# Inverting the tiles of a whole head with pairs of tiles as diagonal blocks of one 128-column stationary operand

## The chip, the cores and the metric

The kernel runs on one core of one Trainium2 chip. The metric is the device time of one launch in microseconds (us), the median over several runs; a lower number is better. Everything said of the hardware here is read from the profile of the kernel's own execution.

## The reference

The program is a two-layer decoder trunk on 1024 positions of width 1024. The first layer mixes positions with a gated DeltaNet of 8 heads (head size 128), the second with a state-space layer ("S5") of 64 groups of 16 channels; beside each runs a cross-attention into 256 memory tokens, and after each comes an MLP with 4096 hidden channels. Two pieces matter here.

In the DeltaNet, each head's sequence is cut into chunks, and each chunk needs the inverse of a unit lower triangular matrix:

```
a_strict = where(strict, einsum('bhnid,bhnjd->bhnij', kb, k) * decay, 0)
sol = triangular_solve(eye + a_strict, rhs, left_side=True, lower=True, unit_diagonal=True)
...
state, o = scan over chunks   # each chunk uses its part of sol
```

The kernel works with chunks of 128 positions, so a head has 8 such 128x128 matrices ("tiles"). In the S5 layer the output of a position has a skip term, `y = y + d_skip * u`.

## The kernel before, in words

All large products are split into a high and a low part (fp32r) and take three matmuls (lines L367 to L369, in `mm3`). The small products of the DeltaNet and the S5 set-up are plain fp32 matmuls; in the trace each of them appears as two MATMUL records and two LDWEIGHTS records.

The program first loads x, projects keys, computes the memory attention, and then goes through the 8 DeltaNet heads. For a head h, `gdn_recur(h)` (the scan over the 8 tiles) is woven with `gdn_fill(h + 1)`, which projects queries, values and the gate of the next head (and keys of the head after) and, between the projection steps, inverts the tiles of head h + 1 (`gdn_invert_tiles`). After the last head follow the output projection, the MLP, the S5 layer and the second MLP. In the first MLP, `s5_side` prepares the S5 matrices beside the large products (`s5_mats`, 16 calls).

The inverses of the 32x32 diagonal blocks of the tiles are computed on VectorE by `gdn_inverse`, for two heads at a time (0 and 1, 2 and 3, ...), and left in DRAM (`t32`, plain and transposed; `ntf` holds the negated strict part of the tiles). `gdn_invert_tiles` joins these blocks: first two 32-blocks to a 64-block, then two 64-blocks to the 128-tile. Each join is a product of the off-diagonal block with the two inverses. Before the change it goes through the four tiles of one half of a head (`hf` = 0, then 1) in five steps; each step, `mm4`, is a group of four matmuls, one for each tile, with 64 stationary and 64 moving columns into one PSUM bank (tag `pi`, one buffer, shared with the transposes `ot`), followed by one or two small copies on ScalarE and VectorE that place the result for the next step. Ten such groups make a head, 80 the program. Names: `lead`, `unit` and `pair` are three 128x512 tiles in the buffers `h4` (six of them), made once at the start and called `bd` in the profile; `nt` holds the off-diagonal blocks; `TT` (called `iv`, as the PSUM bank is too) receives the inverse and is read by `gdn_recur`.

In `s5_mats`, `pz` is a product of four matmuls with 16 stationary columns (one group of channels each) and 128 moving ones; the skip term, a 16x16 diagonal from `dd`, is added to it, and the 16 rows go to DRAM (`zd`) in one transfer of the GpSimd queue.

The order of the instructions on every engine is not that of the code. When the whole program has been recorded, `settle` plans it: each instruction has a cost (`price`) and a due time, TensorE may take matmuls up to 40 us ahead of their turn (`reach=40`), and every engine is then given its order as a chain. Within its engine an instruction then waits for those ahead of it. Tiles of one tag are given out in the recorded order.

Of the kernel before, what the change touches and what calls it, by code (L numbers as in the profile page):

```python
# [30 lines left out]
class Trunk:  # L31
# [26 lines left out]
    def settle(self, first, last, reach=0.0, ahead=15.0, passes=1, margin=0.0, late=0.0, hold=1e3):  # L58
# [10 lines left out]
        ins = traced[k0:k1]  # L69
        n = len(ins)  # L70
# [39 lines left out]
        reads, writes, users, fresh, cost, port = {}, {}, {}, [], [], []  # L110
# [709 lines left out]
    def gdn_consts(self):  # L820
        nc = self.nc
        scr = self.tile("scr", [P, 9 * P], F32, "scr")[:, :P + 8 + 13 * 64 + 96]
        self.small = [scr[:, P + 8 + n * 64:P + 8 + (n + 1) * 64] for n in range(13)]
        early = self.tile("h1", [P, 3 * P], F32, "early")
        U = early[:, 0:P]
        nc.gpsimd.memset(U, 1.0)
        nc.gpsimd.affine_select(U, U, [[1, P]], ALU.is_ge, 0.0, base=0, channel_multiplier=-1)
        self.U = U
        ones = early[:, P:2 * P]
        nc.gpsimd.memset(ones, 1.0)  # L830
        self.ones = ones
        mn = scr[:, 0:P]
        nc.gpsimd.memset(mn, 0.0)
        nc.gpsimd.affine_select(mn, mn, [[1, P]], ALU.is_ge, -1e30, base=0, channel_multiplier=-1)
        self.maskneg = mn
        self.early = [early[:, 2 * P + 64 * n:2 * P + 64 * (n + 1)].rearrange("p (t h) -> p t h", t=8) for n in range(2)]
        self.lead, self.unit, self.pair = (self.tile("h4", [P, 4, P], F32, "bd") for _ in range(3))
        for o in (self.lead, self.pair):
            nc.gpsimd.memset(o, 0.0)
        nc.gpsimd.memset(self.unit, 0.0)  # L840
        for r, c in ((0, 0), (32, 64), (64, 32)):
            nc.scalar.copy(self.unit[r:r + 32, :, c:c + 32], self.ident[r:r + 32, r:r + 32].unsqueeze(1).to_broadcast([32, 4, 32]))
# [285 lines left out]
    def blocks(self, o, h, hf, w, places):  # L1128

        for b, c in places:  # L1130
            q = slice(32 * b, 32 * b + 32)
            self.nc.sync.dma_start(o[q, :, c:c + 32], self.t32[w, h, 4 * hf:4 * hf + 4, b].rearrange("t i c -> i t c"))

    def gdn_invert_tiles(self, h):

        nc = self.nc
        V = nc.vector
        T32, zi = self.lead, self.unit
        B = self.pair.rearrange("p t (w c) -> p w t c", w=2)
        A, B = B[:, 0], B[:, 1]  # L1140

        def mm4(a, b):
            ps = self.psum("pi", "iv", (P, 4, P))[:64, :, 0:64]
            for t in range(4):
                nc.tensor.matmul(ps[:, t], a[:, t], b[:, t], start=True, stop=True)
            return ps

        out = self.TT[h] = []
        for hf in range(2):
            NT = self.tile("h4", [P, 4, P], F32, "nt")  # L1150
            for o, c, w in ((0, 64, 64), (64, 32, 32)):
                nc.sync.dma_start(NT[:, :, o:o + w], self.ntf[h, hf][:, :, c:c + w])
            TT = self.tile("h3", [P, 4, P], F32, "iv")
            nc.gpsimd.memset(TT, 0.0)
            self.blocks(T32, h, hf, 0, ((0, 0), (2, 32)))
            self.blocks(TT, h, hf, 1, ((0, 0), (1, 32), (2, 64), (3, 96)))
            out.append(TT)
            ps = mm4(NT[:, :, 32:96], T32[:, :, 0:64])
            nc.scalar.copy(zi[32:64, :, 0:32], ps[32:64, :, 0:32])
            V.tensor_copy(zi[96:128, :, 32:64], ps[0:32, :, 32:64])  # L1160
            yield 0.5
            ps = mm4(TT[:, :, 0:64], zi.rearrange("p t (w c) -> p t w c", c=32)[:, :, 0:3:2])
            nc.scalar.copy(A[0:64], ps)
            yield 0.5
            ps = mm4(zi[:, :, 0:64], TT.rearrange("p t (w c) -> p t w c", c=32)[:, :, 1:4:2])
            nc.scalar.copy(TT[0:32, :, 32:64], ps[0:32, :, 0:32])
            V.tensor_copy(TT[64:96, :, 96:128], ps[32:64, :, 32:64])
            yield 0.5
            ps = mm4(NT[:, :, 0:64], A)
            nc.scalar.copy(B[64:128], ps)  # L1170
            yield 0.5
            ps = mm4(B, TT[:, :, 64:128])
            nc.scalar.copy(TT[0:64, :, 64:128], ps)
            yield 0.5

    def gdn_queries_out(self, h, hf):

# [533 lines left out]
    def s5_mats(self, m, b, co, banks):  # L1711

        nc = self.nc
# [8 lines left out]
        dd = self.dd(8 * m + 4 * b)  # L1722
        pz = self.psum(banks[0], "pz", (P, 4, 8, 16))
        for g in range(4):
            nc.tensor.matmul(flat(pz[:16, g]), co[:, 0, 4 * b + g, :], flat(h1[:, g]), start=True, stop=True)
        z = self.tile("h5", [P, 4, 8, 16], F32, "z")[:16]
        nc.scalar.copy(z[:, :, 1:8], pz[:16, :, 1:8])
        V.tensor_tensor(z[:, :, 0], pz[:16, :, 0], dd, op=ALU.add)  # L1728
        nc.gpsimd.dma_start(self.zd[m, :, gs, 112:], z.rearrange("p g e o -> p g (e o)"))
# [82 lines left out]
    def s5_read(self, m, u, rs, M0, H):  # L1812

        nc = self.nc
        for b, r in enumerate(rs):
# [9 lines left out]
    def dd(self, g0):  # L1825

        nc = self.nc
        o = self.tile("S", [P, 4, 16], F32, "dd")
        nc.vector.tensor_tensor(o[:16], self.ident[:16, :16].unsqueeze(1).to_broadcast([16, 4, 16]),
                                self.dsk[:, g0:g0 + 4].unsqueeze(2).to_broadcast([16, 4, 16]), op=ALU.mult)  # L1830
        return o[:16]

    def glu(self):
        nc = self.nc
# [194 lines left out]
    def run(self):  # L2029
        nc = self.nc  # L2030
        a = self.a
        d = lambda n, shape: self.dp.tile(shape, F32, tag=n, name=n)
        self.dsk = self.const("dsk", [16, 64])
        nc.sync.dma_start(self.dsk, a["dskT"])
        self.gdn_consts()
        self.s5_scratch()

        self.cat = d("cat0", [1536, T])
# [153 lines left out]
def layouts(x):  # L2192
# [33 lines left out]
    o["dskT"] = c(x["s5_d"].reshape(64, 16).T)  # L2226
# [25 lines left out]
```

## Time and profile before

| | before |
|---|---|
| median of 3 runs | 2619.41 us (2617.07 to 2619.64) |
| profiled execution: time / span | 2622.83 us / 2621.1 us |
| mean granted TensorE clock | 0.993 |
| TensorE matmul busy | 2553.5 us (97%) |
| VectorE / ScalarE / GpSimd busy | 1929.3 us (74%) / 1304.3 us (50%) / 338.1 us (13%) |

In the rows of the profile, PE is TensorE's matmuls, PEld its weight loads, DVE VectorE, ACT ScalarE, POOL GpSimd and SP SyncE, which issues most transfers; a name with a q at its end (SPq, POOLq) is the sequencer of that engine. A row of the timeline gives the start, the length, the engine, the line and operation, the tiles written and read, the size of the operand and the count of equal instructions that were merged. "128*64 128x64" in a matmul row means 128 rows by 64 stationary columns, and a moving operand of 128 partitions by 64 columns. The ends of matmuls are modelled and overlap the next start, so the cost of a matmul on TensorE is read from start to start.

### The profile page before, as it was taken

Reading aid. Unit: us, or ns where it says so; the run is one execution under the profiler, and the core shown is the slowest. Engines: PE = TensorE matmul, PEld = TensorE weight load, DVE = VectorE, ACT = ScalarE, POOL = GpSimd, SP = SyncE. Lnnn points to the kernel's source line nnn. Section 1 sums busy time; section 2 is a strip of 40 time slices with the busy share of each in tenths; the row PEclk is TensorE's granted clock in tenths of the full one; section 3 lists DMA queues with packets and bytes.
Section 4 is the critical chain, followed back from the end, with each engine's and each line's share of the span. In section 5 each row is a group of like instructions: output and inputs, shape, how many; then the busy total and the mean of one; then the engine's idle time right before and its main releaser. Section 6 shows DMA issues by size and latency. Waiting matters only on the chain.

```text
span 2621.1 us, 36895 instructions
## 1 busy us (share of the span) xinstructions
PE 2553.5 (97%) x12621; PEld 2092.7 (80%) x12621; DVE 1929.3 (74%) x3576; ACT 1304.3 (50%) x2930; POOL 338.1 (13%) x478
## 2 busy tenths in 40 slices
PE   8999999999999999999999999999999999999998
PEld 6888787887887787787878888878887788888886
DVE  6674757565768798879988965663768766578778
ACT  6666665664426455544444245663236445454441
POOL 1111112111003003311110122211002000000002
PEclk9999999999999999999999999999999999999999
DMA  5442434343422556677453377655323444574432
GB/s 192 121 121 86 118 94 110 99 131 108 157 89 98 179 183 201 203 256 265 138 169 130 139 245 222 200 167 181 114 79 121 173 161 156 192 271 149 147 105 93
DMA packets 266029, 404.05 MB, mean 154 GB/s; under 512 B 108481, under 2 KB 125073, under 8 KB 265841
## 3 DMA queue, kind: packets, MB, share of 16 engines
q1 hardware_dynamic: 245488, 348.76, 40.7%
q0 software_dynamic: 18048, 48.75, 6.2%
q10 hardware_dynamic: 2304, 4.20, 0.4%
q8 instruction: 99, 1.62, 0.3%
q14 instruction: 90, 0.73, 0.1%
HBM read 274.20 MB, written 127.37 MB: 153 GB/s over the span
## 4 chain that ended last, share of the span: by engine, by line
PE 78%; DVE 10%; issue 4%; ACT 3%; DMA 2%; POOL 2%; SPq 0%; DVEq 0%; POOLq 0%; ACTq 0%
PE q L367 6%; PE q L368 6%; PE q L369 6%; PE tm L367 3%; PE tm L369 3%; PE tm L368 3%; PE pB L367 3%; PE pB L368 3%; PE pB L369 3%; PE wi L367 3%; PE wi L368 2%; PE wi L369 2%; PE pC L367 2%; PE pC L369 2%; PE pC L368 2%
## 5 line engine op out<-in xcount | busy, mean ns | idle before, releaser
L367 PE MATMUL q<-wkh,hkh 128*128 128x512 f32 x784 | 306.8, 392 | 1.0 <-DVE z L1728 0.9
L368 PE MATMUL q<-wkl,hkh 128*128 128x512 f32 x784 | 305.8, 390 | 0.5 <-DVE wkl L778 0.5
L369 PE MATMUL q<-wkh,hkl 128*128 128x512 f32 x784 | 305.5, 390 | 0.0
L777 ACT CAST wkh<-wr 128x512 fp32r<-128x512 f32 x168 | 104.9, 624 | 243.9 <-PE q L368 196.3
L367 PEld LDWEIGHTS q<-wkh,hkh 128*128 128x128 f32 x784 | 147.2, 188 | 33.9 <-issue 2.6
L368 PEld LDWEIGHTS q<-wkl,hkh 128*128 128x128 f32 x784 | 147.2, 188 | 31.5 <-DVE wkl L778 1.1
L369 PEld LDWEIGHTS q<-wkh,hkl 128*128 128x128 f32 x784 | 147.2, 188 | 31.0 <-issue 0.4
L778 DVE TENSOR_TENSOR wkl<-wr,wkh 128x512 fp32r<-128x512 f32 x168 | 115.8, 689 | 64.7 <-issue 51.8
L367 PE MATMUL wi<-xTh,wih 128*128 128x512 f32 x384 | 159.1, 414 | 2.8 <-ACT qT L975 2.8
L369 PE MATMUL wi<-xTh,wil 128*128 128x512 f32 x384 | 153.8, 401 | 0.0
L368 PE MATMUL wi<-xTl,wih 128*128 128x512 f32 x384 | 153.2, 399 | 0.0
L482 POOL TENSOR_SCALAR mv<-mv 128x1 f32<-128x1 f32 x32 | 24.8, 774 | 871.5 <-DVE mv L481 631.1
L778 DVE TENSOR_TENSOR hkl<-hr,hkh 128x512 fp32r<-128x512 f32 x196 | 134.2, 685 | 2.0 <-ACT hkh L777 1.9
L1521 DVE TENSOR_TENSOR y<-tm,y 128x512 f32<-128x512 f32 x128 | 88.0, 689 | 60.4 <-PE tm L369 58.5
L777 ACT CAST hkh<-hr 128x512 fp32r<-128x512 f32 x196 | 120.8, 616 | 1.0 <-DMA hr<-hd 1.0
L367 PEld LDWEIGHTS wi<-xTh,wih 128*128 128x128 f32 x384 | 72.8, 190 | 16.7 <-ACT qT L975 3.1
L369 PEld LDWEIGHTS wi<-xTh,wil 128*128 128x128 f32 x384 | 72.8, 190 | 14.2
L368 PEld LDWEIGHTS wi<-xTl,wih 128*128 128x128 f32 x384 | 72.9, 190 | 12.7 <-issue 0.3
L771 DVE TENSOR_TENSOR y<-q,y 128x512 f32<-128x512 f32 x112 | 72.4, 683 | 0.0
L367 PE MATMUL tm<-ow,ok 128*128 128x512 f32 x160 | 63.6, 397 | 0.0
L369 PE MATMUL tm<-ow,ok 128*128 128x512 f32 x160 | 62.5, 391 | 0.0
L368 PE MATMUL tm<-ow,ok 128*128 128x512 f32 x160 | 62.3, 390 | 0.0
(542 smaller groups left out, 7459.5 us busy)
## 6 DMA issues: line engine op xcount, KB each, us to landing
hr<-hd SPq DMA_DIRECT2D x212, 256.0 KB, 2.7
wr<-in_w_dram SPq DMA_DIRECT2D x56, 512.0 KB, 4.4
hd<-u SPq DMA_DIRECT2D x92, 256.0 KB, 2.0
w1r<-in_w_dram SPq DMA_DIRECT2D x40, 512.0 KB, 3.8
w1r<-in_w_dram SPq DMA_DIRECT2D x64, 256.0 KB, 4.4
hd<-hid SPq DMA_DIRECT2D x60, 256.0 KB, 3.1
hd<-p SPq DMA_DIRECT2D x60, 256.0 KB, 2.5
wir<-in_w_in_dram SPq DMA_DIRECT2D x24, 512.0 KB, 3.8
```

What stands on the lines that cost most here:

```text
L367: mm(ps, a[0], b[0], start=start, stop=False, skip_group_check=onto)
L368: mm(ps, a[0], b[1], start=False, stop=False, skip_group_check=onto)
L369: mm(ps, a[1], b[0], start=False, stop=stop, skip_group_check=onto)
L482: nc.gpsimd.tensor_scalar(mv[:, 2:3], mv[:, 1:2], 1e-5, None, op0=ALU.add)
L771: V.tensor_tensor(o, bank[t], o, op=ALU.add)
L777: nc.scalar.copy(hi, s)
L778: nc.vector.tensor_tensor(lo, s, f32(hi), op=ALU.subtract)
L1521: nc.vector.tensor_tensor(y[c], ps, y[c], op=ALU.add)
```

## The change

`gdn_invert_tiles` takes both halves of a head at once. Tile t of the first half and tile t of the second become two diagonal blocks of one 128x128 stationary operand (four 32-blocks in the first three steps, two 64-blocks in the last two), so each step is one group of four matmuls for all 8 tiles: 128 stationary columns, 32 moving columns in steps 1 to 3 and 64 in steps 4 and 5. Five groups make a head, 40 the program. The block-diagonal operands are six 128x512 tiles in the `h4` buffers (`bz`, `bv`, `na`, `sp`, `tv`, `mz`), made at the first inversion rather than at the start; they are filled by 34 transfers a head on SP where there were 16, and by twelve small copies of a head's second and third step. The steps are spread over the fill of a head by `each = (total - wait) / 5.5`.

In `s5_mats`, `pz` uses all 128 channels of `co[:, 0]` as stationary columns for each of its four matmuls, so each gives eight groups' rows of which 16 are used; the skip comes from a mask (`same`, made once by a reduction of the identity) times a column of `dsk`; the rows used lie on different partitions, so `zd` is written by four transfers where there was one.

In `settle`, an instruction that opens a tile now also counts as due before the next one that opens a tile of the same tag (`taker`).

```diff
-        held, next_ = {}, [[] for _ in ins]
+        held, next_, taker = {}, [[] for _ in ins], {}
         for x in range(n):
+            for k in {self.home[nm][:2] for nm in fresh[x]}:
+                if k in taker:
+                    next_[taker[k]].append(x)
+                taker[k] = x
...
-        self.lead, self.unit, self.pair = (self.tile("h4", [P, 4, P], F32, "bd") for _ in range(3))
-        for o in (self.lead, self.pair):
-            nc.gpsimd.memset(o, 0.0)
-        nc.gpsimd.memset(self.unit, 0.0)
-        for r, c in ((0, 0), (32, 64), (64, 32)):
-            nc.scalar.copy(self.unit[r:r + 32, :, c:c + 32], self.ident[...])
+        self.pieces = None
...
     def gdn_invert_tiles(self, h):
+        if not self.pieces:
+            self.pieces = [self.tile("h4", [P, 4, P], F32, nm) for nm in ("bz", "bv", "na", "sp", "tv", "mz")]
+            for o in self.pieces[:5]:
+                nc.gpsimd.memset(o, 0.0)
...
+        TT = self.TT[h] = [self.tile("h3", [P, 4, P], F32, "iv") for _ in range(2)]
+        for f in range(2):
+            nc.gpsimd.memset(TT[f], 0.0)
+        for k in range(4):
+            f, r = k // 2, 64 * (k % 2)
+            load(bz[q32[k], :, q32[k]], self.ntf[h, f][r:r + 32, :, r + 32:r + 64])
+        for k in range(4):
+            load(m1[q32[k]], block(0, k // 2, 2 * (k % 2)))
+            load(bv[q32[k], :, q32[k]], block(1, k // 2, 2 * (k % 2) + 1))
...
+        ps = mm4(bz, m1, 32)
+        nc.scalar.copy(zc, ps)
+        yield 0.9
+        ps = mm4(bv, zc, 32)
+        for f in range(2):
+            nc.scalar.copy(tA[q32[2 * f + 1], :, q32[0]], ps[q32[2 * f]])
+        for k in range(4):
+            V.tensor_copy(bz[q32[k], :, q32[k]], zc[q32[k]])
+        yield 0.9
+        ps = mm4(bz, m3, 32)
...
+        ps = mm4(na, tA, 64)
...
+        ps = mm4(sp, vB, 64)
...
-        each = (total - wait) / 10.5
+        each = (total - wait) / 5.5
...
-            nc.tensor.matmul(flat(pz[:16, g]), co[:, 0, 4 * b + g, :], flat(h1[:, g]), start=True, stop=True)
+            nc.tensor.matmul(flat(pz[:, g]), flat(co[:, 0]), flat(h1[:, g]), start=True, stop=True)
...
-        nc.gpsimd.dma_start(self.zd[m, :, gs, 112:], z.rearrange("p g e o -> p g (e o)"))
+        for g in range(4):
+            nc.gpsimd.dma_start(self.zd[m, :, 4 * b + g, 112:], flat(z[16 * (4 * b + g):16 * (4 * b + g) + 16, g]))
```

Two places show how the order moves. The first is TensorE in the inversion of head 2, beside the recurrence of head 1 (`wi` is a projection, `qk` the product of queries and keys, `po` belongs to the recurrence). Before:

```order
L367 MATMUL wi_3355<-xTh_14_134,wih_3257 128x512
L1145 MATMUL iv_3275<-bd_90,iv_3236 64x64
L1199 MATMUL qk_3349<-qT_3031,kT_276 128x128
L1145 MATMUL iv_3275<-bd_90,iv_3236 64x64 x3
L1199 MATMUL qk_3349<-qT_3031,kT_276 128x128 x3
L1145 MATMUL iv_3309<-iv_3236,bd_90 64x64 x4
L368 MATMUL wi_3355<-xTl_15_135,wih_3257 128x512
L369 MATMUL wi_3355<-xTh_14_134,wil_3258 128x512
```

Now:

```order
L1163 MATMUL iv_3280<-mz_1964,bz_1959 128x32 x4
L1311 MATMUL po_3331<-S_3297,gb_2772 128x128
L373 MATMUL wi_3370<-xTh_11_126,wil_3231 128x512
L371 MATMUL wi_3370<-xTh_11_126,wih_3230 128x512
L372 MATMUL wi_3370<-xTl_12_127,wih_3230 128x512
L1163 MATMUL iv_3337<-mz_1964,bv_1960 128x32 x4
```

Each group of four has kept its place between the projections, but there are five of them where there were ten, and none is cut: on the whole of TensorE the groups stand in 91 pieces before (one of the eleven that are cut is above, a single `iv` matmul ahead of the first `qk`) and in 40 now.

The second place is SP, with the loads for the same inversion, which begin when `gdn_inverse` has left the blocks of heads 2 and 3 in DRAM (`t`). Before:

```order
L337 DMA wir_3753<-in_w_in_dram 128x1024
L1132 DMA bd_89<-t_106 32x4x32 x2
L987 DMA gb_3186<-gcd 128x512
L1132 DMA iv_3236<-t_106 32x4x32 x4
L1132 DMA bd_89<-t_106 32x4x32 x2
L1028 DMA kdd<-kd_3208 128x512
L1190 DMA Dq_3343<-ded 128x512
L987 DMA gb_3345<-gcd 128x512
L1152 DMA nt_4073<-ntf 128x4x64
L1152 DMA nt_4073<-ntf 128x4x32
L1132 DMA bd_89<-t_106 32x4x32 x2
L1132 DMA iv_3417<-t_106 32x4x32 x4
```

Now:

```order
L341 DMA wir_3758<-in_w_in_dram 128x1024
L1148 DMA mz_1964<-t_97 32x4x32 x4
L1149 DMA bv_1960<-t_97 32x4x32 x4
L1153 DMA mz_1964<-t_97 32x4x32
L1151 DMA tv_1963<-t_97 32x4x32 x4
L1154 DMA tv_1963<-t_97 32x4x32
```

Before, two loads serve the first step, and the 16 of a head stand among other loads (`gb`, `Dq`, `kdd`). Now the last two rows alternate until there are four of each; the two loads of `na` and the first four of `iv` follow, so that 26 loads stand one behind the other ahead of the next one for other work; the four of `bz`, which do not need `t`, stand ahead of this place.

More of the change, by code (lines that the diff above doesn't have):

```diff
@@ L1126, in gdn_inverse @@
             nc.gpsimd.dma_start(dst[0][:, 16:32, 8 * y:8 * y + 8], Tn[q])
[L1128 to L1132, printed above, removed]
     def gdn_invert_tiles(self, h):
         nc = self.nc
[L1137 to L1143, printed above, removed]
+        V, load = nc.vector, nc.sync.dma_start
@@ new lines, in gdn_invert_tiles @@
+        if not self.pieces:
+            self.pieces = [self.tile("h4", [P, 4, P], F32, nm) for nm in ("bz", "bv", "na", "sp", "tv", "mz")]
+            for o in self.pieces[:5]:
+                nc.gpsimd.memset(o, 0.0)
+        bz, bv, na, sp, tv, mz = self.pieces
+        tA, vB = (tv.rearrange("p t (w c) -> p w t c", w=2)[:, w] for w in range(2))
+        m1, m3, zc = (mz.rearrange("p t c -> p (t c)")[:, w * P:(w + 1) * P].rearrange("p (t c) -> p t c", t=4) for w in range(3))
+        q32 = [slice(32 * k, 32 * k + 32) for k in range(4)]
@@ new lines, in gdn_invert_tiles @@
+        q64 = [slice(64 * k, 64 * k + 64) for k in range(2)]
+        block = lambda x, hf, b: self.t32[x, h, 4 * hf:4 * hf + 4, b].rearrange("t i c -> i t c")
+        TT = self.TT[h] = [self.tile("h3", [P, 4, P], F32, "iv") for _ in range(2)]
[7 more added lines that the diff above has]
+            load(bv[q32[k], :, q32[k]], block(1, k // 2, 2 * (k % 2) + 1))
@@ new lines, in gdn_invert_tiles, with mm4 @@
+        for k in range(4):
+            load(tA[q32[k], :, q32[k % 2]], block(0, k // 2, k % 2))
+        for k in range(4):
+            load(m3[q32[k]], block(1, k // 2, 2 * (k % 2) + 1))
+            load(vB[q32[k], :, q32[k % 2]], block(1, k // 2, 2 + k % 2))
+        for f in range(2):
+            load(na[q64[f], :, q64[f]], self.ntf[h, f][0:64, :, 64:P])
+            for b in range(4):
+                load(TT[f][q32[b], :, q32[b]], block(1, f, b))
+        def mm4(a, b, n):
+            ps = self.psum("pi", "iv", (P, 4, P))[:, :, 0:n]
@@ L1146, in mm4 @@
             return ps
[L1148 to L1174, printed above, removed]
+        ps = mm4(bz, m1, 32)
+        nc.scalar.copy(zc, ps)
+        yield 0.9
+        ps = mm4(bv, zc, 32)
+        for f in range(2):
+            nc.scalar.copy(tA[q32[2 * f + 1], :, q32[0]], ps[q32[2 * f]])
+        for k in range(4):
+            V.tensor_copy(bz[q32[k], :, q32[k]], zc[q32[k]])
+        yield 0.9
+        ps = mm4(bz, m3, 32)
+        for f in range(2):
+            V.tensor_copy(vB[q32[2 * f], :, q32[1]], ps[q32[2 * f + 1]])
+            V.tensor_copy(TT[f][q32[0], :, q32[1]], ps[q32[2 * f]])
+            nc.scalar.copy(TT[f][q32[2], :, q32[3]], ps[q32[2 * f + 1]])
+        yield 0.9
+        ps = mm4(na, tA, 64)
+        for f, copy in enumerate((nc.scalar.copy, V.tensor_copy)):
+            copy(sp[q64[f], :, q64[f]], ps[q64[f]])
+        yield 0.9
+        ps = mm4(sp, vB, 64)
+        for f, copy in enumerate((nc.scalar.copy, V.tensor_copy)):
+            copy(TT[f][q64[0], :, q64[1]], ps[q64[f]])
+        yield 0.9
     def gdn_queries_out(self, h, hf):
@@ L1721, in s5_mats @@
         nc.gpsimd.dma_start(self.h1d[m, :, gs, 8:9], h8)
-        dd = self.dd(8 * m + 4 * b)
+        dd = self.tile("S", [P, 1, 16], F32, "dd")
+        V.tensor_scalar(dd[:, 0], self.same, self.dsk[:, m:m + 1], None, op0=ALU.mult)
         pz = self.psum(banks[0], "pz", (P, 4, 8, 16))
         for g in range(4):
[L1725 to L1729, printed above, removed]
+            nc.tensor.matmul(flat(pz[:, g]), flat(co[:, 0]), flat(h1[:, g]), start=True, stop=True)
+        z = self.tile("h5", [P, 4, 8, 16], F32, "z")
+        nc.scalar.copy(z[:, :, 1:8], pz[:, :, 1:8])
+        V.tensor_tensor(z[:, :, 0], pz[:, :, 0], dd.to_broadcast([P, 4, 16]), op=ALU.add)
+        for g in range(4):
+            nc.gpsimd.dma_start(self.zd[m, :, 4 * b + g, 112:], flat(z[16 * (4 * b + g):16 * (4 * b + g) + 16, g]))
         g1 = self.combine(co[:, 0], co[:, 1], re[:, 0:8, gl], im[:, 0:8, gl], b, "G1T")
@@ L1823, in s5_read @@
             nc.sync.dma_start(self.yd[m].rearrange("s (o g) n -> (s o) g n", o=16)[:, 4 * b:4 * b + 4, :], zg)
[L1825 to L1831, printed above, removed]
     def glu(self):
@@ L2032, in run @@
         d = lambda n, shape: self.dp.tile(shape, F32, tag=n, name=n)
-        self.dsk = self.const("dsk", [16, 64])
+        dsk = self.const("dsk", [P, 64])
+        self.dsk, self.same = dsk[:, 0:8], dsk[:, 8:24]
         nc.sync.dma_start(self.dsk, a["dskT"])
         self.gdn_consts()
+        nc.vector.tensor_reduce(self.same, self.ident.rearrange("p (g o) -> p o g", o=16), axis=AX.X, op=ALU.add)
         self.s5_scratch()
@@ L2225, in layouts @@
     o["c1"], o["c2"] = c(np.concatenate(d, 0)), c(np.concatenate(d[::-1], 0))
-    o["dskT"] = c(x["s5_d"].reshape(64, 16).T)
+    o["dskT"] = c(x["s5_d"].reshape(8, 128).T)
     o["w_glu"] = tiles(x["s5_w_glu"][0][swap][:, swap])
```

1 line of the change is left out of this document (removed).

## The prediction

> **What bounds the kernel now.** I read the page first, then the windows of the DeltaNet heads, where all the inversions lie, then what TensorE waits for there, and last the timeline of single groups. The page:
>
> ```profile
> span 2621.1 us, 36895 instructions
> PE 2553.5 (97%) x12621; PEld 2092.7 (80%) x12621; DVE 1929.3 (74%) x3576; ACT 1304.3 (50%) x2930; POOL 338.1 (13%) x478
> PE 78%; DVE 10%; issue 4%; ACT 3%; DMA 2%; POOL 2%; SPq 0%; DVEq 0%; POOLq 0%; ACTq 0%
> ```
>
> TensorE is busy 97% of the span and holds 78% of the chain that ended last. An average says nothing of a stage, so here are three windows between the first inversion (183 us) and the last (670 us); the columns after the length are busy times of PE, PEld, DVE, ACT and POOL:
>
> ```profile
> 183.00:278.00 95.00, 95.00 (x582) 76.76 (x582) 55.51 (x114) 58.25 (x186) 9.80 (x14) 1.00 0.33 96
> 278.00:419.00 141.00, 138.45 (x820) 113.89 (x819) 90.36 (x180) 89.42 (x298) 24.09 (x32) 0.99 0.39 108
> 559.00:670.00 111.00, 108.78 (x660) 88.28 (x660) 65.07 (x118) 57.61 (x186) 12.14 (x16) 0.98 0.45 130
> ```
>
> PE is busy for 98 to 100% of each, DVE and ACT for 52 to 64%. And the waits of TensorE from 183 to 670 us, of whose seven rows these are the first and the last (us in total, times, longest):
>
> ```profile
> PE wi L367 <- ACT qT L975: 2.8, 2, 1.4
> PE pe L1300 <- DVE R L1296: 0.4, 1, 0.4
> ```
>
> No row exceeds 2.8 us in 487 us. TensorE's own sequence sets the pace here, so TensorE time taken out of this stage should come off the span, as long as no new wait takes its place.
>
> **The inversion.** What does a group of four matmuls cost on TensorE today? The time is read from start to start:
>
> ```profile
> 183.18 0.40 PE L367 MATMUL wi<-xTh,wih 128*128 128x512 f32 x1
> 183.51 0.68 PE L1145 MATMUL iv<-bd,nt 128*64 128x64 f32 x8
> 184.12 0.50 PE L368 MATMUL wi<-xTl,wih 128*128 128x512 f32 x1
> 184.46 0.40 PE L369 MATMUL wi<-xTh,wil 128*128 128x512 f32 x1
> 184.69 0.39 PE L367 MATMUL wi<-xTh,wih 128*128 128x512 f32 x1
> ...
> 320.33 0.33 PE L1145 MATMUL iv<-bd,iv 128*64 128x64 f32 x2
> 321.00 0.56 PE L1145 MATMUL iv<-bd,iv 128*64 128x64 f32 x6
> ```
>
> Two wide matmuls in a row start 0.23 us apart (184.46 to 184.69). From 183.18 to 184.12 pass 0.94 us, of which 0.23 belong to the `wi` ahead, so 0.71 to the group; the `wi` behind it takes 0.34 instead of 0.23, another 0.11. A group therefore costs 0.82 us, and 80 of them 65.6 us. Where another matmul cuts a group (the last two rows), two entries and exits are paid: 0.82 less the 0.47 that eight records need at 0.058 (below) leaves 0.35, and eleven groups are cut, 3.8 us. Together 69.4 us go to inversions now.
>
> After the change each record has 128 stationary columns. No group in this trace has that with 32 or 64 moving columns in this place, but `gc` and `gl` have it near the start, four records in all, 64 moving columns:
>
> ```profile
> 38.27 0.39 PE L368 MATMUL wi<-xTl,wih 128*128 128x512 f32 x1
> 38.62 0.41 PE L935 MATMUL gc<-early 128*128 128x64 f32 x2
> 38.86 0.39 PE L936 MATMUL gl<-early 128*128 128x64 f32 x2
> 39.06 0.48 PE L369 MATMUL wi<-xTh,wil 128*128 128x512 f32 x1
> 39.37 0.39 PE L367 MATMUL wi<-xTh,wih 128*128 128x512 f32 x1
> ...
> 38.59 0.30 PEld L935 LDWEIGHTS gc<-early 128*128 128x128 f32 x2 [0.35 <-issue]
> 183.51 0.54 PEld L1145 LDWEIGHTS iv<-bd,nt 128*64 128x64 f32 x8 [0.37 <-issue]
> 21.12 0.32 PEld L893 LDWEIGHTS bat<-ident,baT 32*128 32x128 f32 x4 [0.44 <-issue]
> ```
>
> From 38.27 to 39.06 is 0.79, less 0.23 is 0.56; the `wi` behind takes 0.31, 0.08 more. Four records cost 0.64. Their pace is that of the weight load, not of the 64 moving columns: a load of 128 columns lasts 0.19 (two end after 0.30, so they start 0.11 apart), while the 64-column loads of the eight `iv` records, 0.135 long, start (0.54 - 0.135)/7 = 0.058 apart. Eight records then cost 0.64 + 4 x 0.11 = 1.08 us, and 40 groups 43.2 us. That is 26.2 us less, and the reader should see what it consists of: records fall from 640 to 320, but each takes twice as long (640 x 0.058 = 37 us against 320 x 0.11 = 35 us). Nearly all of the gain is in entering and leaving fp32 groups among fp32r matmuls 40 times instead of 91.
>
> The Trainium skill, page "TensorE: Matmul & The Clock Gate", section "LDWEIGHTS (loading the stationary operand)", says this in general: a load takes P/1.2 ns for P columns, whatever the rows. That is 107 ns at 128 columns and 53 at 64, so it speaks against the change: the same time in loads for half as many groups; the trace agrees with 0.11 and 0.058. It differs on rows: the last row above has four loads of 32 rows by 128 columns in 0.32, about half the time of full ones.
>
> That row bounds the other side. If the 32-column groups (24 of the 40) ran at its pace, (0.32 - 0.135)/3 = 0.06, each would be 8 x 0.05 = 0.4 us cheaper, 9.6 us in all. I take 0.11, since the stationary operand here has all 128 rows as `gc` has.
>
> **The copies and the loads.**
>
> ```profile
> L1159 ACT COPY bd<-iv x16: 256/256/258, 184.2 to 646.2; 32x128 f32<-32x128 f32 x16
> L1160 DVE COPY bd<-iv x16: 282/284/286, 184.6 to 647.0; 32x128 f32<-32x128 f32 x16
> L1163 ACT COPY bd<-iv x16: 365/366/368, 186.2 to 654.8; 64x256 f32<-64x256 f32 x16
> ```
>
> A head had ten ACT copies and four on DVE; it now has seven and ten (by the order of the two kernels, ACT has 29 instructions fewer and DVE 49 more in all). Six more DVE copies of about 0.28 us are 1.7 us a head, on an engine that is idle for more than a third of each window: nothing. If that cover were gone, 14 us for eight heads.
>
> The loads are the new risk. They wait for `gdn_inverse` in the even heads:
>
> ```profile
> 311.84 0.79 SPq L1132 DMA_DIRECT2D bd<-t  x2
> 351.32 0.49 PE L1300 MATMUL pe<-mix,iv 128*128 128x128 f32 x2
> L1132 SPq DMA_DIRECT2D iv<-t x64: 302/430/570, 163.1 to 650.8; - x64
> DMA to landing us min/median/max: 1.5/1.9/4.3
> ```
>
> Head 2's blocks can be loaded from 311.84, and its recurrence starts at 351.32. The 26 loads now issued there take 26 x 0.43 = 11.2 us and the last lands by about 327; five groups at some 2 us follow, and they begin before the last load. That fits into the 39.5 us. But `price` counts 0.33 for an issue, so the plan may set a group up to 26 x 0.10 = 2.6 us too early, and TensorE, which keeps its order, would stand there with the projections queued behind; SP's `Dq`, `gb` and `wir` come later by as much. Three even heads (2, 4, 6) wait so: 0 to 8 us; I take 3. Waiting for both halves before a recurrence instead of for one is in the plan already: the order moves other matmuls ahead.
>
> **S5 and the start.**
>
> ```profile
> 1126.55 0.39 PE L368 MATMUL pC<-xB,s4h 128*128 128x512 f32 x1
> 1126.87 1.05 PE L1725 MATMUL pz<-H,co 128*16 128x128 f32 x8
> 1127.84 0.50 PE L369 MATMUL pC<-xB,s4l 128*128 128x512 f32 x1
> L1729 POOL DMA_DIRECT2D zd<-z x16: 527/528/551, 1072.2 to 1413.3; - x16
> POOL zd L1729 <- DVE z L1728: 116.9, 9, 24.3
> ...
> 7.56 0.91 ACT L842 COPY bd<-ident 32x128 f32<-32x128 f32 x3
> 8.49 5.51 ACT L869 CAST xTh<-x 128x512 fp32r<-128x512 f32 x10
> ```
>
> A `pz` group costs 1.29 - 0.23 = 1.06 us up to the next start. Its 128 moving columns set that, and 128 stationary columns, by `gc`, load at the same pace: between -1 and +1 us for 16 groups, I take 0. The mask costs DVE no more than `dd` did. Three more `zd` transfers a call are 48 x 0.53 = 25 us on POOL, in a stage where POOL itself waited 116.9 us for `z`: hidden. At the start, the three ACT copies of 0.91 us that stood right ahead of the first cast of x are gone, and the first matmuls wait for that cast: -0.5, between 0 and -0.9.
>
> **The sum** against the profiled execution of 2622.83 us: -26.2 + 3 - 0.5 = -23.7, so about 2599. It ran 3.4 us above the median of the runs; against the median of 2619.41 the forecast is 2596. The order has also been planned anew in other stages (`taker`, other costs); TensorE's waits there can come out a few us better or worse, which I count as +-6 on everything. The measurement can tell from no change about 0.2%, 5 us.
>
> **The rivals.**
> 1. *Loads are short at 32 moving columns*: 9.6 us more gain, 2586. For it the 32-row loads, against it `gc`. 10%.
> 2. *Half of it comes back*: a recurrence or the chain of `gdn_inverse` becomes the limit in the even heads, so that only the odd ones get shorter. Half of 26.2 less 3: 2609. For it, an even head's blocks are ready 39.5 us ahead of its recurrence whatever TensorE does; against it, inversions need less than 20 of these. 12%.
> 3. *Only the loads count*: if the time at the entries into fp32 groups is paid elsewhere once the groups are gone, 37 us against 35 remain, and with the 3 us of late loads it is no change, 2619 to 2620. Against it, the 0.1 us that is seen on both sides of each group. 6%. (The Trainium skill's rule by columns, on the page named above, is this rival when nothing else is counted.)
> 4. *SP becomes the limit*: one load queue serves the heads; 18 more loads a head are 18 x 0.43 = 7.7 us, and `wir` for the projections stands behind loads that wait for the buffers of the last inversion (`bz` is free only after step three). If all of that reaches TensorE in all eight heads, +62 - 26, so 2655; it decides from 3.3 us a head on. Against it: the odd heads' blocks lie ready for a whole head, and SP's 34 loads are 15 us of some 70 (the second window holds two heads). 8%.
>
> The forecast itself gets 64%. The low end is rival 1 with 3 us of better order, 2583; the high end is rival 2 with 3 us on top, 2612. Faster by over 0.2%: forecast, rivals 1 and 2, less a little for their upper tails, 84%; within 0.2%, rival 3 and that tail, 8%; slower 8%.
>
> **What would show it.** In the changed profile, `iv` should have 320 records in 40 groups at some 1.1 us from the wide matmul ahead to normal pace behind, its weight loads 0.11 apart; the stage from the first to the last inversion should be about 20 to 25 us shorter, with TensorE's waits there still below some 12 us in all. `pz` groups should stay near 1.06 us. A `iv` or `wi` matmul that waits for a DMA, repeatedly in the even heads, would speak for the fourth rival; loads 0.06 apart for the first. The forecast is wrong if the stage is shorter by less than 12 us, or if other stages move by more than 10.

## The result, and the profile after

The changed kernel takes 2601.69 us (median of 4 runs, 2600.03 to 2604.86); before, on the same chip, 2618.77 (2617.07 to 2619.64). The ratio is 0.9937, with a 95% interval of 0.992 to 0.9954: 17 us faster, 12 to 21 by the interval. The forecast was 2596, in a range from 2583 to 2612.

The page of the changed kernel, in the lines that were shown of before:

```profile
span 2603.1 us, 36577 instructions
PE 2522.5 (97%) x12301; PEld 2093.2 (80%) x12301; DVE 1941.7 (75%) x3625; ACT 1294.7 (50%) x2901; POOL 362.3 (14%) x528
PE 75%; DVE 11%; ACT 4%; DMA 2%; issue 2%; POOL 2%; SPq 1%; POOLq 0%; DVEq 0%; ACTq 0%
```

TensorE is still the bound, with 31 us less work. Where did the 18 us of the span come from? Grouped rows give the first and last start of a kind of matmul, and so the ends of stages. The first inversion, the last `pe` (end of the recurrences) and the last `py` (after the first MLP and the S5 set-up), first of before, then of after:

```profile
L1145 PE MATMUL iv<-bd,nt x256: 222/222/271, 183.5 to 662.4; 128*64 128x64 f32 x128
L1300 PE MATMUL pe<-R,iv x112: 270/274/421, 219.6 to 735.5; 128*128 128x128 f32 x112
L1820 PE MATMUL py<-r,H x128: 274/275/421, 1555.1 to 1735.8; 128*128 128x127 f32 x128
```

```profile
L1163 PE MATMUL iv<-mz,bz x128: 190/276/352, 190.1 to 637.0; 128*128 128x32 f32 x128
L1314 PE MATMUL pe<-R,iv x112: 270/273/562, 221.5 to 727.2; 128*128 128x128 f32 x112
L1836 PE MATMUL py<-r,H x128: 274/275/421, 1534.7 to 1713.8; 128*128 128x127 f32 x128
```

The first inversion starts 6.6 us later (183.5, 190.1). From there to the last `pe` it takes 537.1 us in place of 552.0, a gain of 14.9. From `pe` to the last `py` 986.6 in place of 1000.3, a gain of 13.7 in a stage where the forecast had none. The rest of the program is 4 us longer.

In the DeltaNet stage a group of the new inversion looks like this, matmuls first, then their weight loads:

```profile
202.63 0.39 PE L372 MATMUL wz<-xTl,wzh 128*128 128x512 f32 x1
202.86 0.39 PE L373 MATMUL wz<-xTh,wzl 128*128 128x512 f32 x1
203.09 1.00 PE L1163 MATMUL iv<-tv,na 128*128 128x64 f32 x8
203.89 0.48 PE L371 MATMUL wz<-xTh,wzh 128*128 128x512 f32 x1
204.21 0.39 PE L372 MATMUL wz<-xTl,wzh 128*128 128x512 f32 x1
...
202.86 1.08 PEld L1163 LDWEIGHTS iv<-tv,na 128*128 128x128 f32 x8
```

The eight records keep the predicted pace: from 203.09 to the next start pass 0.80, and record by record the starts lie 0.11 apart (the wide one follows the last sooner). What is missing is the entry. The `wz` ahead (202.86) is followed at its usual 0.23, because the first load already ran beside it; the old group had 0.33 there and a bubble of 0.37 in front of its load. A group costs 0.80 + 0.09 behind it (0.32 to the next `wz` instead of 0.23), so 0.89 us, not 1.08; the median over the groups is the same (0.81 for the old ones).

But new waits have come. TensorE from 183 to 670 us (in total, times, longest):

```profile
PE pS L1320 <- ACT e L1316: 4.4, 2, 2.2
PE pS L1320 <- DMA kdl<-kdd: 3.9, 1, 3.9
PE iv L1163 <- DMA mz<-t: 2.6, 1, 2.6
PE iv L1163 <- ACT iv L1179: 1.9, 2, 1.6
```

and the longest of its waits up to the first inversion that was not there before:

```profile
PE kt L1014 <- DVE kT L979: 7.1, 1, 7.1
```

The nine rows of the stage sum to 17 us, where seven summed to 7; the prediction had named 12 as the limit. The loads of `mz` come late in an even head, as it feared, and `kdl`, which the recurrence needs, stands on SP behind this burst and the first loads for the next head. A second measure, used below, adds up what each start on TensorE comes later than the pace of the matmul ahead asks (0.23 us for 512 columns, 0.11 for an fp32 record of 128), where that is over 0.25 us. Between the first inversion and the last `pe` this is 10.4 us before and 23.8 after. Some 20 of the 23.8 lie within 50 us from 290, 440 and 590 us, where heads 2, 4 and 6 are inverted.

### The profile page after: what moved, and what is told of

It reads as the page before. It is cut to its first block, busy times and chain, and to the rows that moved or that the text cites. A ratio compares the mean times of both kernels' runs of the same rounds, so it can differ in the third digit from the quotient of the medians.

```text
span 2603.1 us, 36577 instructions
## 1 busy us (share of the span) xinstructions
PE 2522.5 (97%) x12301; PEld 2093.2 (80%) x12301; DVE 1941.7 (75%) x3625; ACT 1294.7 (50%) x2901; POOL 362.3 (14%) x528
## 4 chain that ended last, share of the span: by engine, by line
PE 75%; DVE 11%; ACT 4%; DMA 2%; issue 2%; POOL 2%; SPq 1%; POOLq 0%; DVEq 0%; ACTq 0%
PE q L372 6%; PE q L371 6%; PE q L373 6%; PE tm L371 3%; PE tm L373 3%; PE tm L372 3%; PE pB L371 3%; PE pB L372 3%; PE pB L373 3%; PE wi L371 2%; PE wi L373 2%; PE wi L372 2%; PE pC L371 2%; PE pC L372 2%; PE pC L373 2%
```

## The experiments

**One part at a time.** Four kernels, each timed against the kernel before. First settle's rule alone:

```diff
 (kernel before)
+            for k in {self.home[nm][:2] for nm in fresh[x]}:
+                if k in taker:
+                    next_[taker[k]].append(x)
+                taker[k] = x
```

> The kernel before with one edit of the change alone: settle's new rule, by which an instruction that takes a buffer of a ring is also ordered behind the one that took that ring before it; inversion and pz are the old ones. Theory (the change's gain is in the two groups of matmuls, its losses at the start and in the DeltaNet stage are loads of the new inversion that come late): the rule by itself changes next to nothing, 2617 to 2621 us against 2618.8, first inversion matmul at 183 to 185 us as in the kernel before. Rival (the planner's order makes both the +6.6 us ahead of the first inversion and some 6 us of the gain in the first MLP): with the rule alone the first inversion matmul comes at 188 to 191 us, and the time is 2612 (gain without loss), 2625 (loss without gain) or, with both, about 2619 with the milestones moved.

Measured: 2618.83 us, ratio 0.9991 (0.9982 to 1.0), so between nothing and 5 us. But inside the profile it is not nothing; here is one row of TensorE's waits, then the three kinds of matmul that mark the stages:

```profile
PE kt L1019 <- DVE kT L984: 7.1, 1, 7.1
```

```profile
L1149 PE MATMUL iv<-bd,nt x256: 221/222/271, 187.1 to 668.1; 128*64 128x64 f32 x128
L1304 PE MATMUL pe<-R,iv x112: 270/274/415, 223.4 to 740.9; 128*128 128x128 f32 x112
L1824 PE MATMUL py<-r,H x128: 273/275/421, 1550.5 to 1729.6; 128*128 128x127 f32 x128
```

The wait of 7.1 us on `kT` is the rule's. VectorE makes `kT` at nearly the same time (57.33 us before, 57.66 now), but the tile `kv`, which it made before that (53.53), now comes behind it (58.94), and so do the `mk` matmuls that had filled TensorE from 54.01 to 59.91. The first inversion is 3.6 us later by it. The last `pe` is 5.4 us later than before, and from there to `py` it takes 988.7 us, 11.6 less. The rival was right that both marks move, though the first by less than it said (187.1, not 188 to 191): most of the changed kernel's gain in the first MLP comes with an order, not with a cheaper operation.

`pz` alone, without the rule:

```diff
 (kernel before)
-            nc.tensor.matmul(flat(pz[:16, g]), co[:, 0, 4 * b + g, :], flat(h1[:, g]), start=True, stop=True)
+            nc.tensor.matmul(flat(pz[:, g]), flat(co[:, 0]), flat(h1[:, g]), start=True, stop=True)
 ... (the mask, the copies and the four transfers too)
```

> The kernel before with only pz changed: 128 stationary columns in place of 16 and the skip from the mask; the old inversion, and settle without the new rule. Theory (a group of matmuls with a narrow stationary operand pays about 0.09 us ahead of its first and 0.11 us behind its last, one with 128 columns does not): a group of four costs 0.90 us in place of 1.18, x16 = -4.5 us, so 2614.3 us. Rival (what the prediction said: the pace of the records, 0.11 x 4 to 0.24 x 4, hides the columns, pz 0): 2618.8. Second rival (the 10.8 us that the changed kernel gains in the first MLP all come from pz, through the stalls that its wait for the old groups made): 2608.

Measured: 2615.78 us, ratio 0.9982 (0.9973 to 0.9991), 4.7 us faster. Its group, to be held against that of before in the prediction (1126.55 to 1127.84):

```profile
1126.29 0.39 PE L369 MATMUL pC<-xB,s4l 128*128 128x512 f32 x1
1126.52 1.05 PE L1726 MATMUL pz<-H,co 128*128 128x128 f32 x8
1127.33 0.48 PE L367 MATMUL pC<-xB,s4h 128*128 128x512 f32 x1
1127.64 0.40 PE L368 MATMUL pC<-xB,s4h 128*128 128x512 f32 x1
```

Before, 1.29 us passed from the wide matmul ahead to the one behind; now 1.04, and 0.31 after it, where 0.34 passed behind the old narrow groups (184.12 to 184.46 in the prediction). That is 0.28 us for each of 16 groups, the 4.5 of the theory.

The inversion with the rule (old `pz`), and the changed kernel without the rule:

> The changed kernel with the old pz and the old skip; inversion and settle's rule are the new ones. Theory (narrow groups pay at entry and exit): pz's 4.5 us come back, 2606.2 us, DeltaNet stage as in the changed kernel. Rival (pz costs the same either way): 2601.7. Second rival (all 10.8 us of the first MLP are pz's): 2612.5.

> The changed kernel without settle's new rule. Theory (the rule is free): 2600 to 2604 us and the same marks, first inversion matmul near 190 us. Rival (the rule, not the new loads, puts the wait of 7.1 us on kT at 52 us): the wait is gone, first inversion matmul at 183 to 185 us, and the time is 2594 to 2597. Second rival (the rule keeps two of the inversion's tiles from waiting on each other): waits on DMAs of bz, m1, tA or m3 grow by over 5 us in the DeltaNet stage and the time is over 2607.

The third gave 2607.16 us, ratio 0.9942 (0.993 to 0.9955). The median is 1 us from the theory's 2606.2, but the kernel before was slower beside these runs as well (2621.07). By the ratios, next to the whole change (0.9937), `pz` is left 1 us, and the two intervals allow from -4 to 7; so the 4.7 us are shown for `pz` alone and neither shown nor excluded for `pz` in company. The fourth gave 2618.39 us, ratio 0.9989 (0.998 to 0.9998): without the rule nearly all of the gain is gone. The waits from 183 to 735 us say where:

```profile
PE pS L1316 <- ACT e L1312: 9.4, 7, 4.0
PE pS L1316 <- DMA kdl<-kdd: 4.5, 1, 4.5
...
PE iv L1159 <- DMA mz<-t: 2.7, 1, 2.7
PE qk L1209 <- DVE mix L1210: 2.1, 2, 1.1
```

The inversion's matmuls cost the same as with the rule; the stalls over 0.25 us are 34.8 us instead of 23.8, and the stage takes 548.3 us, 11.2 more. The first MLP takes 11.7 us more as well (last `pe` at 734.2, last `py` at 1732.5). A first inversion that comes 4.2 us earlier makes up for a part of both. The theory that the rule is free fell. The first rival was right that the wait for `kT` goes without the rule, and wrong on the time; the second had the time right, but not the place: the loads of `mz` wait as before, and it is the recurrence (`pS`) that waits twice as long for ScalarE's copy `e`. Why that copy stands later in the plan without the rule was not taken further.

**What a group costs by its shape.** `pz` in the changed kernel was done twice, in 15 of its 16 calls with another shape beside the full one:

```diff
+        for rows, cols in ([full, (r, w)] if last else [(r, w), full]):
             for g in range(4):
-                nc.tensor.matmul(flat(pz[:, g]), flat(co[:, 0]), flat(h1[:, g]), start=True, stop=True)
+                nc.tensor.matmul(flat(pz[:cols, g]), flat(co[:rows, 0])[:, :cols], flat(h1[:rows, g]), start=True, stop=True)
```

> The changed kernel with pz computed twice, as a probe: in 15 of its 16 calls four more matmuls of another shape (16, 32, 64, 96, 112, 120 or 127 stationary columns over 128 rows, or 32, 64, 96 or 112 rows by 128 columns) stand ahead of the four full ones, which write the same bank again, or behind them (16, 64, 112 and 96 columns). What is read is the time from the wide matmul ahead to the first narrow record, and from the last narrow record to the wide one behind; the kernel's own time only rises by some 0.9 us a call. Theory (only a load of the full 128 columns and 128 rows is taken ahead of the running matmul): every shape below 128 columns shows some 0.09 us ahead of its first record, 112 and 127 as much as 16, and 128 columns 0.00. Rival (the cost grows smoothly with the columns that are missing): 112 and 127 show under 0.02, 64 some 0.05. For fewer rows at 128 columns the theory says nothing: 0.00 would mean that columns decide alone, 0.09 that the whole array has to be filled.

The one run took 2617.06 us. Four of the calls, with 64, 96 and 112 stationary columns and with 64 rows ahead of the eight full records (the x16 merges both):

```profile
1110.99 0.39 PE L371 MATMUL pB<-xB,a4h 128*128 128x512 f32 x1
1111.31 2.18 PE L1745 MATMUL pz<-H,co 128*64 128x128 f32 x16
1113.24 0.48 PE L372 MATMUL pB<-xB,a4h 128*128 128x512 f32 x1
...
1144.71 0.39 PE L373 MATMUL pB<-xB,s3l 128*128 128x512 f32 x1
1144.94 1.93 PE L1745 MATMUL pz<-H,co 128*96 128x128 f32 x16
1146.63 0.47 PE L371 MATMUL pB<-xB,a4h 128*128 128x512 f32 x1
...
1150.62 0.39 PE L371 MATMUL pB<-xB,a4h 128*128 128x512 f32 x1
1150.85 1.93 PE L1745 MATMUL pz<-H,co 128*112 128x128 f32 x16
1152.53 0.47 PE L372 MATMUL pB<-xB,a4h 128*128 128x512 f32 x1
...
1250.80 0.39 PE L371 MATMUL q<-wkh,hkh 128*128 128x512 f32 x1
1251.12 2.24 PE L1745 MATMUL pz<-H,co 64*128 64x128 f32 x16
1253.12 0.47 PE L372 MATMUL q<-wkl,hkh 128*128 128x512 f32 x1
```

and the loads of two of them, with the idle time ahead in brackets:

```profile
1111.30 0.85 PEld L1745 LDWEIGHTS pz<-H,co 128*64 128x64 f32 x8 [0.35 <-ACT s2h L547]
1112.32 0.97 PEld L1745 LDWEIGHTS pz<-H,co 128*128 128x128 f32 x8 [0.17 <-issue]
...
1150.62 1.97 PEld L1745 LDWEIGHTS pz<-H,co 128*112 128x112 f32 x16
```

With 64 columns the wide matmul ahead is followed after 0.32 us, its load starts only as the matmul ahead is left, and there is another gap of 0.17 where the columns change to 128; from wide to wide 2.25 us. With 96 or 112 columns it is followed after 0.23, sixteen loads run without a gap, and 1.92 and 1.91 us pass. So both theories were wrong: the price is neither bound to exactly 128 columns nor does it grow with what is missing. It is a step: 16, 32 and 64 columns show 0.09 us ahead of the first record, 96, 112, 120 and 127 under 0.01, and rows do the same (0.09 at 32 and 64, none at 96 and 112). The Trainium skill has the rule that this fits, on the page "TensorEngine Tiling (Array Packing)", section "Tiling Modes": the array has modes of 128, 64 and 32 rows or columns, and "Changing tiling mode (not just tile) drains the TensorE". The step between 64 and 96 agrees with it, though no row of the trace names a mode. By that rule the old inversion and the old `pz` changed the mode twice for each group.

**Where the stalls come from.** Four orders that were to be rid of them: the rule only from the first inversion on; 0.43 us as the planner's price of an issue on SP; both; and the `kdl` loads on GpSimd's queue, without and with that price.

```diff
+            begun = begun or any(nm.startswith("iv") for nm in fresh[x])
-            for k in {self.home[nm][:2] for nm in fresh[x]}:
+            for k in {self.home[nm][:2] for nm in fresh[x]} if begun else ():
...
-            return (0.33 if i.engine != E.Pool else 0.65), ...
+            return (0.43 if i.engine == E.SP else 0.33 if i.engine != E.Pool else 0.65), ...
...
-            nc.sync.dma_start(kd[hf], self.kdd[h, hf])
+            nc.gpsimd.dma_start(kd[hf], self.kdd[h, hf])
```

> The changed kernel with settle's new rule only from the first instruction that opens an inversion tile on; ahead of it the order is that of the kernel without the rule. Theory (the rule costs some 4 us at the start, through the wait of 7.1 us on kT, saves some 11 us in the DeltaNet stage and some 6 in the first MLP): first inversion matmul at 185 to 187 us in place of 190, all else as in the changed kernel, 2596 to 2599 us. Rival (the stalls depend on the whole order, so a new start deals them anew): 2600 to 2606.

> The changed kernel with the planner's price of a transfer issued on SP raised from 0.33 to the 0.43 us that the trace shows. Theory (the waits of TensorE on the loads of m3 and kdl, 2.6 and 3.9 us in head 6, come from a plan that takes 34 issues for 3.4 us shorter than they are): both waits fall below 1 us in all, 2594 to 2597 us. Rival (SP has no later free time there, so the plan only moves the wait elsewhere, or other stages lose what this one gains): 2600 to 2606 with other waits in their place.

> Both edits, the rule from the first inversion on and 0.43 us for an issue on SP. Theory (they act in different stages and add): 2590 to 2594 us. Rival (the planner deals new stalls for each order): 2598 to 2606.

> The changed kernel with the two kdl loads of a head issued on the queue of GpSimd, which is busy 14%, in place of SP's. Theory (kdl comes late in head 6 only because it is queued behind the inversion's burst on SP): the wait of 3.9 us goes, 2597 to 2599 us. Rival (the planner puts them as late on any queue, or the new order costs as much elsewhere): 2600 to 2605.

> The changed kernel with 0.43 us as the price of an issue on SP and the kdl loads on the queue of GpSimd. Theory (with the dear price alone 5.0 us of waits on kdl remained; they go): 2592 to 2595 us. Rival (they come back as other waits): 2597 to 2600, as with the dear price alone.

| | median us | ratio to before | first inversion at | stalls over 0.25 us in the stage |
|---|---|---|---|---|
| the change | 2601.69 | 0.9937 (0.992 to 0.9954) | 190.1 | 23.8 |
| rule late | 2607.61 | 0.9955 (0.9942 to 0.9969) | 186.1 | 26.2 |
| 0.43 for an issue | 2598.41 | 0.9915 (0.9902 to 0.9929) | 189.8 | 21.9 |
| both | 2597.76 | 0.9915 (0.9901 to 0.9928) | 185.5 | 22.3 |
| `kdl` on GpSimd | 2600.63 | 0.9932 (0.9919 to 0.9944) | 188.5 | 25.3 |
| `kdl` on GpSimd, 0.43 | 2600.13 | 0.9926 (0.9914 to 0.9939) | 189.3 | 21.8 |

The start can be had back (4 us in two of them), and each wait can be moved, but the stalls stay between 22 and 26 us. That is what the rivals said. Of their times only that of `kdl` on GpSimd was met; two versions are just above (2607.61 for up to 2606, 2600.13 for up to 2600) and the two with 0.43 us and `kdl` on SP between theory and rival. With the dear price the wait for `mz` falls from 2.6 to 1.2 us, and `kdl` is late in two other heads (waits of that kernel, 183 to 735 us):

```profile
PE pS L1320 <- DMA kdl<-kdd: 5.0, 2, 3.1
...
PE iv L1163 <- DMA mz<-t: 1.2, 2, 0.8
```

The two versions with 0.43 us and `kdl` on SP have the lowest medians of those that change nothing of the computation, 21 us under before and 3 to 4 us under the change, which the intervals don't separate.

**What the late blocks cost.** In the even heads `gdn_inverse` leaves its 32-blocks late, so here the loads take blocks that have long been there. First for everything, then for the operands of the groups alone. Both kernels leave out part of the computation: the blocks of heads 2 to 7 are replaced by those of heads 0 and 1, so their inverses are not the right ones.

```diff
-        block = lambda x, hf, b: self.t32[x, h, 4 * hf:4 * hf + 4, b]...
+        block = lambda x, hf, b, h=h % 2: self.t32[x, h, 4 * hf:4 * hf + 4, b]...
 (the second of the two only:)
-                load(TT[f][q32[b], :, q32[b]], block(1, f, b))
+                load(TT[f][q32[b], :, q32[b]], block(1, f, b, h))
```

> The changed kernel, but the inversion of every head reads the 32-blocks of heads 0 or 1, which lie in DRAM long before, so that no load of them waits for gdn_inverse (the inverses of heads 2 to 7 are then not theirs). What is measured is the prediction's term for late loads, put at 3 us there. Theory (the late blocks cause the waits on m3 and, through the burst behind them, on kdl, and force groups close together, 2.6 + 3.9 + 1.9 us): stalls over 0.25 us between the first inversion and the last recurrence fall from 23.8 to some 15 us, 2592 to 2596 us. Rival (the stalls are ScalarE's and the plan's, and come with five denser groups in any case): 20 us or more of stalls, 2599 to 2604.

Measured: 2600.91 us, ratio 0.9929 (0.9916 to 0.9943), stalls 25.1: the time of the rival. But of the stalls one is this:

```profile
PE ks L1308 <- DVE S L1325: 9.6, 1, 9.6
```

It lies at head 7's recurrence, behind `gdn_inverse`'s last work, which nobody reads in this kernel any more and which the plan therefore put off. Up to there the kernel was 18 us ahead of the change. Hence the second:

> The changed kernel where only the operands of the groups (bz, m1, bv, tA, m3, vB) take the 32-blocks of heads 0 or 1; the diagonal blocks of the inverse itself, which the recurrence reads, are still the head's own, so gdn_inverse has to be done in time as in the changed kernel, only not for the groups (the inverses of heads 2 to 7 are then wrong off the diagonal). It tells apart what the run before it left mixed: there gdn_inverse had no reader from the third head on, its last work was put off into head 7's recurrence, which waited 9.6 us for it, while up to that point the stretch from the first inversion to head 7's recurrence took 458.4 us against 475.0 in the changed kernel and 489.8 before. Theory (the late blocks, through the loads and the groups pushed behind them, hold back some 13 to 17 us of the gain): the stretch takes 458 to 464 us, and without that wait the time is 2588 to 2592. Rival (it is gdn_inverse's own work on VectorE and ScalarE that stands in the way of the recurrence, in whatever order the loads come): the stretch stays at 470 to 475 us, 2598 to 2603.

Measured: 2586.64 us, ratio 0.9872 (0.9856 to 0.9889). The theory holds, by a little more than it asked (2588 to 2592). The ends of the stage, then the waits from 183 to 735 us:

```profile
L1163 PE MATMUL iv<-mz,bz x128: 190/276/276, 188.9 to 617.6; 128*128 128x32 f32 x128
L1314 PE MATMUL pe<-R,iv x112: 270/273/357, 220.3 to 707.9; 128*128 128x128 f32 x112
```

```profile
PE po L1311 <- ACT on L1339: 2.5, 3, 1.0
...
PE pS L1320 <- DMA kdl<-kdd: 0.7, 1, 0.7
PE pS L1320 <- ACT e L1316: 0.7, 1, 0.7
```

The last `pe` starts 519.1 us after the first inversion, 32.9 less than before, with 10.5 us of stalls, as many as before. No stretch of 50 us has more than 2.3 us of stalls left. With early blocks even the waits of `pS` for `e` and `kdl` fall from 4.4 and 3.9 us to 0.7 each, and no reordering had moved that for `e`. They go with the late blocks. This kernel's plan is another one too, but the change and five other plans of it had left 21.8 us or more; by which path the blocks hold up `e` was not followed.

## Why the prediction was right or wrong

The number was right within 6 us, and the bound (TensorE's own sequence, so that its time comes off) was right. By its own test, though, the forecast was wrong: the first MLP moved by 13.7 us, where it allowed 10. The stage became shorter by 14.9 us, above its limit of 12 but short of 20 to 25, and its waits came to 17 us, not below 12. Errors of both signs met, so that the number is in part luck.

1. *The price of a group*, 1.08 us, so -26.2. Pace and count were right (320 records in 40 groups), the entry was not: 0.89 us, 35.6 in all, so -34. With early blocks the stage comes near it, -32.9 (up to 3 of which are the clock's, below). The step that failed in this term is the row taken as nearest: the `gc` group stood behind a bubble of 0.35 in its own load row. The new groups, with 128 columns like `gc` and partly with its 64 moving ones, have none, so it was no price of the shape; what it was, the trace does not say (it is marked as issue). The first rival (loads 0.06 apart at 32 columns) was wrong, and so was the third: the time at the entries is not paid elsewhere.
2. *Late loads*, 3 us, 0 to 8. This is the term most mis-sized. Between the change and early operands lie 0.65% of 2620, 17 us, give or take 6 by the two intervals; the stage alone has 18 (537.1 against 519.1), with 13 us of stalls less. The granted clock has a part in it. TensorE's window of the stage, for before, the change and early operands (the third lists more engines; the clock is the third number from the end):

```profile
183.00:735.00 552.00, 544.43 (x3204) 0.99 0.40 114
183.00:735.00 552.00, 534.66 (x2955) 0.98 0.43 120
183.00:735.00 552.00, 545.02 (x3036) 462.70 (x3036) 384.95 (x767) 324.32 (x1055) 76.05 (x98) 1.00 0.45 123
```

   In the change the clock stands at half for 20.5 us of the stage, in four stretches from 315, 452, 605 and 622 us, by the inversions of the even heads; before for 6.8 us, from 314 and 597; with early operands never. That is at most 10, 3 and 0 us lost. The other runs agree, each against the kernel before on the same chip: seven versions with the new inversion and late blocks have mean clocks of 0.990 to 0.994 against 0.994 to 0.998, early operands 0.994 or 0.995 against 0.994 to 0.997. Whether the stalls bring the low clock is not shown, so the 17 us are what late blocks cost with all that comes with them. The second rival, half of it comes back, with the blocks of even heads as its cause, is what happened in this stage; it had 12%. The working counted only the groups that would stand too early by SP's price. It left out what the recurrence loses in waits for its copies `e` and for `kdl`, and the clock.
3. *`pz`*, 0 (+-1). Alone it is -4.7 (2.4 to 7.1). The prediction had quoted the 0.32 us between the wide matmul and the old group and put them down to 128 moving columns.
4. *The start*, -0.5. The first matmul does come 0.7 us earlier (9.2, 8.4), but the first inversion is 6.6 us late. Settle's rule alone, with the wait of 7.1 us for `kT`, makes it 3.6 later, and the change without the rule 2.4 (185.9); where these 2.4 come from was not sought.
5. *The order planned anew*, +-6. The rule alone costs 5.4 us up to the last recurrence and gains 11.6 in the first MLP; and the change without the rule is worth almost nothing (0.9989). It was treated as noise around a sum, and was a condition of that sum.

The fourth rival (SP as the limit, +36) did not come: SP's burst delays single transfers. The terms do not add: -34, 17, -4.7 and -2.4 (the rule alone) make -24, and -17 was measured. Each new order deals the stalls anew; that remainder of 7 us is not settled. The granted clock, which the prediction showed in its windows and gave no term, may also lie in the other stages: over the whole program a mean of 0.991 in 2603 us is 23 us not granted, against 18 before (0.993) and 13 with early operands (0.995); in the first MLP it is 5.1 us against 8.5 before, up to 3 of the 13.7 that were gained there.

## What to carry to other kernels

When small matmuls are mixed into a stream of full ones, ask for each group whether it changes the array's shape: in this case one with up to 64 rows or columns cost 0.28 us more than the same group padded to 96 or more, and padding was free as long as the weight load was not the pace. A gain of TensorE time is worth what the next producer allows: look for the data that comes last (here 32-blocks from VectorE in even heads), and price not only its own wait but what is queued behind it. And where an order is planned, test a planner's edit by itself and left out: here it was worth 0 to 5 us alone, and the change without it 0.5 to 5 of its 17.

## What the runs showed of the hardware that was not expected

The step by shape: matmuls with 16, 32 or 64 stationary columns, or 32 or 64 rows, pay 0.09 us on entry from a full one and again a gap of some 0.2 us in all on the way back to 128; 96, 112, 120 and 127 columns, or 96 and 112 rows, pay neither, and their loads run beside the matmul ahead. Between, at 65 to 95, nothing was measured.

Full fp32 records keep one pace, 0.11 us, for 32, 64 and 128 moving columns (0.80 for eight `iv` records, 0.81 for eight of `pz`), and for 16 to 127 stationary columns in the `pz` probe, too, at 128 moving ones; there the moving operand and not the load is the pace.
